# The entry of the MLP in a hybrid decoder layer: normalisation halves on VectorE, two operands built later, a third pair of hidden tiles started early

## The chip, the cores and the metric

The kernel runs on one core of one Trainium2 chip. The metric is device microseconds of one execution; before the change the median of three runs is 1310.89 us (1308.47 to 1311.84). TensorE (PE in the profile) multiplies into PSUM; VectorE (DVE), ScalarE (ACT) and GpSimd (POOL) do the element work; SyncE (SP) only issues DMAs here. Each engine works through its own instructions in order, so an instruction that waits holds up everything behind it on that engine.

## What is computed

One decoder layer on 1024 tokens of width 1024, in float32. Attention and retention run first; the change touches what comes after them:

```python
y = jnp.concatenate([y_ret, y_dsa], axis=-1)
h = h + y @ w_out[l]                                   # output projection
u = rmsnorm(h, norm2_w[l])                             # second norm
h = h + jnp.square(jax.nn.relu(u @ w_ff1[l])) @ w_ff2[l]   # MLP, 1024 -> 4096 -> 1024
```

## The kernel before

**Precision.** A float32 operand is split in a high half (a rounded copy, made by ScalarE) and a low half (operand minus high half, a subtraction). A product is then three matmuls: high by high, high by low, low by high. Names that end in `h` and `l`, or begin with `wh` and `wl`, are such halves.

**The output projection** (`out_mm`, L689) takes 24 matmuls per block of 128 tokens and column half `ch`: eight slices `d` of `y`, three matmuls each (L694 to L696). Its weights for one column half are loaded as four raw tiles of two slices (`wr`, three buffers) and split into `ow[0]`. `out_prep` loads the four tiles `ys` of a block from DRAM. The list `todo` (last piece of column half 0, then the eight blocks of column half 1) is worked through one after the other.

**The second norm** (`norm2`, L875 on) of block `b` runs between the blocks of the output projection, by `norm_step`. When both column halves of block `b` are in `hrow` (L702), ScalarE squares and sums (L879), GpSimd makes the reciprocal root (two tiny operations, L141 and L142), VectorE scales into `un` (L881), TensorE transposes `un` in eight pieces into two PSUM tiles `tps[0]` and `tps[1]` (L889), and ScalarE and VectorE build from these the operands of the MLP.

**The MLP's first product** uses a scheme with seven products in place of eight, on halves of the tokens (blocks 0 to 3 and 4 to 7) and of the width. Its token operands are `U[m]`, m = 1 to 7. With `tps` of a block b < 4 called x1, x2 and of the block b + 4 called y1, y2: U[2] = x1 and U[4] = x2 - x1 need the first four blocks alone; U[3] = y1 - y2, U[5] = y2, U[6] = y1 + x1, U[7] = y2 + x2 and U[1] = y2 + x1 need the last four too. `f1` keeps x1 and x2 (`g1`, `g2`). All but U[1] are split inside `norm2`; the low halves of U[4], U[3] and U[6] on GpSimd, those of U[2], U[5] and U[7] on VectorE. U[1] is split at units 3 to 6.

**Pairs and units.** The 4096 hidden rows are worked in 16 pairs `p` of 128-row tiles. A unit (`unit1`) is one product m of one pair: four slices, three matmuls each, 12 in all, and then its share in the four results `C[p, "1a"]`, `"1b"`, `"2a"`, `"2b"` by the table `EVAC`: `1` and `-1` are copies by ScalarE (with a sign), `"+"` and `"-"` additions by VectorE. After the last share of a result (`FIN`) ScalarE applies relu and square. `prep1(n)` builds the weight halves of unit n from the raw tiles (`w1_load`), `AHEAD1` = 4 units ahead. The units stand in the order of `groups`:

```python
groups = [(1, ORD[:2]), (0, ORD), (1, ORD[2:])] + [(p, ORD) for p in range(2, NP)]   # ORD = (2, 4, 3, 5, 6, 7, 1)
```

so products 2 and 4 of pairs 1 and 0, four units that need the first four blocks alone, come ahead of the first product 3.

**What sets the order.** The code is recorded once and a scheduler then places each engine's instructions; the order on an engine can therefore differ from the order of the code, and is fixed in the built program. Semaphores carry the dependences.

Of the kernel before, what the change touches and what calls it, by code (L numbers as in the profile page):

```python
# [81 lines left out]
def layer(ctx, tc, x, meta, norm1_w, w_in, ret_w, q_w, k_w, rel, w_out, norm2_w, w1, w2,  # L82
# [603 lines left out]
    def out_w(ch, alt=False):  # L686
        ow[0] = load_cols(w_out, [(512 * ch, 512)], alt=alt, gain=rgain)
# [188 lines left out]
    def norm2(b, src, u):  # L876
# [15 lines left out]
        def halves(m, x, eng):  # L892
            h, l = [v[:, :, s] for v in U[m]]
            nc.scalar.activation(h, x, AF.Copy)
            eng.tensor_tensor(l, x, h.bitcast(F32), op=SUB)

        def temp():
            return p2["p"].tile([128, 4, 128], F32, tag="yd", name="ut", bufs=4)

        def total(m, x, y, op, eng):  # L900
            t = temp()
            nc.vector.tensor_tensor(t, x, y, op=op)
            halves(m, t, eng)
# [90 lines left out]
    def unit1(n):  # L994
# [10 lines left out]
        for q, how in EVAC[m]:  # L1005
            if how in (1, -1):
                tag, k = ("yd", 4) if q in ("1a", "2b") else ("aop", 6)
                C[p, q] = p2["p"].tile([128, 512], F32, tag=tag, name="c" + q, bufs=k)
                nc.scalar.activation(C[p, q], ps, AF.Copy, scale=float(how))
            else:  # L1010
                c = C[p, q]
                nc.vector.tensor_tensor(c, c, ps, op=ADD if how == "+" else SUB)
                if (q, m) in FIN:
                    nc.scalar.activation(c, c, AF.Relu)
                    nc.scalar.activation(c, c, AF.Square)
                    if q in HELD:
                        nc.sync.dma_start(hid[HELD[q]][:, p], c)
# [147 lines left out]
    for n in range(len(units)):  # L1165
# [56 lines left out]
```

## Time and profile before

| what | value |
|---|---|
| median of three runs | 1310.89 us |
| the profiled execution | 1311.07 us, its span on the core 1309.2 us |
| TensorE busy | 1248.5 us (95%) |
| VectorE busy | 1037.7 us (79%) |
| ScalarE busy | 761.3 us (58%) |
| GpSimd busy | 236.2 us (18%) |
| mean granted TensorE clock | 0.98 of full speed |

The page's first part gives an engine's busy time over the whole span. A view by stretches does the same for chosen pieces of the span, with the granted TensorE clock (1.00 is 2.4 GHz) and the load on the DMA engines. The view of waits sums the idle time of an engine by what ended it. The timeline lists instructions with their start; a bracket gives the idle time ahead of one and what ended it. Starts of matmuls that follow each other closely are the reliable figure there; their durations overlap.

### The profile page before, as it was taken

Reading aid. Unit: us, or ns where it says so; the run is one execution under the profiler, and the core shown is the slowest. Engines: PE = TensorE matmul, PEld = TensorE weight load, DVE = VectorE, ACT = ScalarE, POOL = GpSimd, SP = SyncE. Lnnn points to the kernel's source line nnn. Section 1 sums busy time; section 2 is a strip of 40 time slices with the busy share of each in tenths; the row PEclk is TensorE's granted clock in tenths of the full one; section 3 lists DMA queues with packets and bytes.
Section 4 is the critical chain, followed back from the end, with each engine's and each line's share of the span. In section 5 each row is a group of like instructions: output and inputs, shape, how many; then the busy total and the mean of one; then the engine's idle time right before and its main releaser. Section 6 shows DMA issues by size and latency. Waiting matters only on the chain.

```text
span 1309.2 us, 18365 instructions
## 1 busy us (share of the span) xinstructions
PE 1248.5 (95%) x6032; PEld 1031.6 (79%) x6032; DVE 1037.7 (79%) x2297; ACT 761.3 (58%) x1612; POOL 236.2 (18%) x286
## 2 busy tenths in 40 slices
PE   5999989999999899999997999999999999999998
PEld 4888867777887677877786888888888888888887
DVE  5579999995459889976579887777788887887875
ACT  6567556787975777764356565555455444444442
POOL 4002373425244332200233000000000100000000
PEclk8999989999999899999998999999999999999999
DMA  8103031202021322212963444434539834344222
GB/s 277 61 18 91 17 97 63 74 9 73 9 73 39 131 98 83 84 60 89 324 225 119 169 145 153 145 145 144 186 129 345 327 112 181 137 153 173 94 95 97
DMA packets 101278, 165.05 MB, mean 126 GB/s; under 512 B 8712, under 2 KB 48944, under 8 KB 97472
## 3 DMA queue, kind: packets, MB, share of 16 engines
q1 hardware_dynamic: 101184, 163.90, 36.3%
q8 instruction: 47, 0.77, 0.2%
q14 instruction: 47, 0.39, 0.1%
HBM read 113.46 MB, written 51.85 MB: 126 GB/s over the span
## 4 chain that ended last, share of the span: by engine, by line
PE 69%; DVE 18%; ACT 5%; issue 3%; DMA 2%; POOL 1%; SPq 0%; ACTq 0%; DVEq 0%; POOLq 0%
PE psB L1121 5%; PE psB L1120 5%; PE psB L1122 5%; PE psB L1002 4%; PE psB L1003 4%; PE psB L1004 4%; PE psA L1003 4%; PE psA L1002 4%; PE psA L1004 4%; PE psA L246 3%; PE psA L247 3%; PE psA L248 3%; PE psA L1121 3%; PE psA L1120 3%; PE psA L1122 3%
## 5 line engine op out<-in xcount | busy, mean ns | idle before, releaser
L973 ACT ACTIVATE wh<-ga 128x512 fp32r<-128x512 f32 x144 | 87.5, 628 | 164.0 <-PE psB L1121 143.1
L246 PE MATMUL psA<-wh,uh 128*128 128x512 f32 x376 | 152.4, 406 | 2.9 <-DVE fg L487 2.2
L247 PE MATMUL psA<-wh,ul 128*128 128x512 f32 x376 | 150.1, 399 | 0.0
L248 PE MATMUL psA<-wl,uh 128*128 128x512 f32 x376 | 149.8, 399 | 0.0
L974 DVE TENSOR_TENSOR wl<-ga,wh 128x512 fp32r<-128x512 f32 x144 | 96.7, 688 | 49.4 <-ACT wh L973 48.8
L973 ACT ACTIVATE wh<-sum 128x512 fp32r<-128x512 f32 x128 | 78.8, 625 | 71.6 <-DVE sum L970 61.0
L751 ACT ACTIVATE jk_top<-sc,tcand 128x784 bf16<-128x784 f32 (+2 forms) x93 | 98.3, 1057 | 24.4 <-DVE tcand L821 20.3
L1121 PE MATMUL psB<-wh,wl 128*128 128x512 f32 x280 | 108.9, 389 | 0.0
L1122 PE MATMUL psB<-wl,wh 128*128 128x512 f32 x280 | 108.9, 389 | 0.0
L1120 PE MATMUL psB<-wh 128*128 128x512 f32 x280 | 106.8, 389 | 0.0
L974 DVE TENSOR_TENSOR wl<-sum,wh 128x512 fp32r<-128x512 f32 x128 | 88.6, 693 | 4.7 <-ACT wh L973 4.7
L246 PEld LDWEIGHTS psA<-wh,uh 128*128 128x128 f32 x376 | 71.9, 191 | 16.9 <-DVE fg L487 1.9
L248 PEld LDWEIGHTS psA<-wl,uh 128*128 128x128 f32 x376 | 71.7, 191 | 14.0
L247 PEld LDWEIGHTS psA<-wh,ul 128*128 128x128 f32 x376 | 71.8, 191 | 12.5
L1040 POOL COPY ga<-wl 128x1 f32<-128x1 f32 x8 | 6.6, 827 | 400.3 <-PE psB L1003 276.3
L746 DVE TENSOR_SCALAR_CACHE_REDUCE jk_cnt<-sc,tcand 128x400 bf16<-128x400 f32 (+2 forms) x93 | 70.3, 756 | 1.0
L359 ACT ACTIVATE rl<-psB,absw 128x320 f32<-128x320 f32 (+5 forms) x104 | 53.1, 556 | 31.0 <-DVE sc L363 16.8
L1121 PE MATMUL psA<-wh,wl 128*128 128x512 f32 x168 | 65.4, 389 | 0.0
L1122 PE MATMUL psA<-wl,wh 128*128 128x512 f32 x168 | 65.4, 389 | 0.0
L1120 PE MATMUL psA<-wh 128*128 128x512 f32 x168 | 64.9, 389 | 0.0
L194 POOL TENSOR_TENSOR wl<-wr,wh 128x512 fp32r<-128x512 f32 x44 | 61.3, 1419 | 19.0 <-ACT wh L189 15.6
L363 DVE SCALAR_TENSOR_TENSOR sc<-rl,sgnw,sc 128x320 f32<-128x320 f32 (+5 forms) x91 | 56.1, 651 | 8.2 <-ACT rl L359 7.2
(391 smaller groups left out, 3582.0 us busy)
## 6 DMA issues: line engine op xcount, KB each, us to landing
ga<-hid SPq DMA_DIRECT2D x28, 1024.0 KB, 5.2
wr<-in_w_ff_dram SPq DMA_DIRECT2D x34, 512.0 KB, 4.9
hid<-hs SPq DMA_DIRECT2D x48, 256.0 KB, 2.0
wr<-in_w_in_dram SPq DMA_DIRECT2D x32, 256.0 KB, 3.1
ysd<-ys SPq DMA_DIRECT2D x32, 256.0 KB, 2.4
ys<-ysd SPq DMA_DIRECT2D x32, 256.0 KB, 5.0
gb<-in_w_ff_dram SPq DMA_DIRECT2D x8, 1024.0 KB, 5.3
ga<-in_w_ff_dram SPq DMA_DIRECT2D x8, 1024.0 KB, 5.0
```

The source lines that it names most:

```text
L246: nc.tensor.matmul(ps[:P, :n], uh, wh, start=d == 0, stop=False)
L247: nc.tensor.matmul(ps[:P, :n], ul, wh, start=False, stop=False)
L248: nc.tensor.matmul(ps[:P, :n], uh, wl, start=False, stop=d == 7)
L751: nc.scalar.activation(jk_top[:, :ncol[i]], sc[i], AF.Sign, scale=-1.0, bias=cand[:, j:j + 1], accum_out=cnt[:, j:j + 1])
L973: nc.scalar.activation(view(hi), s, AF.Copy)
L974: nc.vector.tensor_tensor(view(lo), s, view(hi).bitcast(F32), op=SUB)
L1002: nc.tensor.matmul(ps, hi[:, a], uh[:, d], start=d == 0, stop=False)
L1003: nc.tensor.matmul(ps, lo[:, a], uh[:, d], start=False, stop=False)
L1004: nc.tensor.matmul(ps, hi[:, a], ul[:, d], start=False, stop=d == 3)
L1120: nc.tensor.matmul(ps[tb], ah[:, t], bh, start=j == 0 and m not in CONT, stop=False, skip_group_check=True)
L1121: nc.tensor.matmul(ps[tb], al[:, t], bh, start=False, stop=False, skip_group_check=True)
L1122: nc.tensor.matmul(ps[tb], ah[:, t], bl, start=False, stop=j == NO - 1, skip_group_check=True)
```

## The change

It is made of six edits.

1. `norm2`: the low halves of U[4], U[3] and U[6] are subtracted on VectorE, none on GpSimd (`halves` has no engine argument any more). GpSimd keeps L141 and L142.
2. `norm2`: U[7] and U[1] are no longer split there and at units 3 to 6; their sums stay in `f1` (`g2` takes y2 + x2 in place). A new function `late_halves` splits them at units 5 to 8, two blocks per unit. A small GpSimd copy that reads the last low half of U[3] and writes into U[7] and U[1] stands ahead of it.
3. `groups`: products 2 and 4 of pair 2 come right behind those of pair 1, so six units stand ahead of the first product 3; the raw weights of pair 2 are loaded twice.
4. `EVAC` and `FIN`: products 2 and 4 are copied out alone, by ScalarE, as `"1b"` and `"1a"`; at product 3 VectorE makes `"2b"` (product 3 minus `"1b"`) and adds `"1a"` to `"1b"`, which is then finished. Per pair ScalarE has three copies in place of four, VectorE as many operations as before, one of them between SBUF tiles.
5. The raw weights of the output projection's second half are loaded ahead of the last block of the first half, and split between the load of the next block.
6. The first raw tiles of the MLP and the first two `prep1` are called up to two blocks earlier.

```diff
-            eng.tensor_tensor(l, x, h.bitcast(F32), op=SUB)
+            nc.vector.tensor_tensor(l, x, h.bitcast(F32), op=SUB)
...
-            total(4, tps[1], g1, SUB, nc.gpsimd)
+            nc.vector.tensor_tensor(t, tps[1], g1, op=SUB)
+            halves(4, t)
         else:
+            nc.scalar.activation(t, tps[0], AF.Copy)
+            nc.vector.tensor_tensor(t, t, tps[1], op=SUB)
+            halves(3, t)
+            halves(5, tps[1])
             t = temp()
-            nc.scalar.activation(t, tps[0], AF.Copy)
-            total(3, t, tps[1], SUB, nc.gpsimd)
-            halves(5, tps[1], nc.vector)
-            total(6, tps[0], g1, ADD, nc.gpsimd)
-            total(7, tps[1], g2, ADD, nc.vector)
+            nc.vector.tensor_tensor(t, tps[0], g1, op=ADD)
+            nc.vector.tensor_tensor(g2, tps[1], g2, op=ADD)
             nc.vector.tensor_tensor(g1, tps[1], g1, op=ADD)
+            halves(6, t)
+
+    def late_halves(m, tb):
+
+        s = slice(128 * tb, 128 * tb + 128)
+        h, l = [v[:, :, s] for v in U[m]]
+        x = f1[m == 7][:, tb]
+        nc.scalar.activation(h, x, AF.Copy)
+        nc.vector.tensor_tensor(l, x, h.bitcast(F32), op=SUB)
...
-    EVAC = {2: [("1b", 1), ("2b", -1)], 4: [("1b", "+"), ("1a", 1)], 3: [("2a", 1), ("2b", "+")], 5: [("2a", "+"), ("1a", "-")],
+    EVAC = {2: [("1b", "=")], 4: [("1a", "=")], 3: [("2a", "="), ("2b", "1b"), ("1b", "1a")], 5: [("2a", "+"), ("1a", "-")],
             6: [("2b", "+")], 7: [("1a", "+")], 1: [("1a", "+"), ("2b", "+")]}
-    FIN = {("1b", 4), ("2a", 5), ("1a", 1), ("2b", 1)}
+    FIN = {("1b", 3), ("2a", 5), ("1a", 1), ("2b", 1)}
-    groups = [(1, ORD[:2]), (0, ORD), (1, ORD[2:])] + [(p, ORD) for p in range(2, NP)]
+    groups = [(1, ORD[:2]), (2, ORD[:2]), (0, ORD), (1, ORD[2:]), (2, ORD[2:])] + [(p, ORD) for p in range(3, NP)]
...
+    for g in range(3):
+        w_out_raw(g)
     for k, (ch, b) in enumerate(todo):
         if k == 1:
-            out_w(1, True)
-        nxt = out_prep(*todo[k + 1]) if k < NB else None
+            ow[0] = [], []
+            for g in range(4):
+                if g == 1:
+                    nxt = out_prep(*todo[k + 1])
+                    w_out_raw(3)
+                w_out_split(g)
+        else:
+            nxt = out_prep(*todo[k + 1]) if k < NB else None
...
-        if k == 6:
+        if k == 5:
             w1_load(0, 0)
             w1_load(0, 1)
-
-    for n in range(2):
-        prep1(n)
+        if k in (6, 7):
+            prep1(k - 6)
...
-        if 3 <= n < 7:
-            s = slice(128 * (n - 3), 128 * (n - 3) + 128)
-            nc.scalar.activation(U[1][0][:, :, s], f1[0][:, n - 3], AF.Copy)
-            nc.vector.tensor_tensor(U[1][1][:, :, s], f1[0][:, n - 3], U[1][0][:, :, s].bitcast(F32), op=SUB)
+        for m, n0 in ((7, 5), (1, 7)):
+            if n == n0:
+                nc.gpsimd.tensor_copy(U[m][0][:, 0, 0:512:128], U[3][1][:, 0, 384:388].bitcast(F32))
+            for tb in (2 * (n - n0), 2 * (n - n0) + 1):
+                if 0 <= tb < 4:
+                    late_halves(m, tb)
```

What it makes of the order in the built programs, at three places. The number behind a name tells buffers apart; they differ between the two programs.

**TensorE where the output projection goes over to column half 1.** `psB_7381` collects block 0 and `psB_7413` block 1; `wh_7368` (before) and `wh_7373` (after) come from the fourth raw weight tile. Before:

```order
L694 MATMUL psB_7381<-wh_7362,ys_5240 128x512
L695 MATMUL psB_7381<-wh_7362,ys_5240 128x512
L696 MATMUL psB_7381<-wl_7363,ys_5240 128x512
L694 MATMUL psB_7381<-wh_7368,ys_5240 128x512
L695 MATMUL psB_7381<-wh_7368,ys_5240 128x512
L694 MATMUL psB_7413<-wh_7338,ys_5236 128x512
```

After, the end of block 1's twelve rows and what follows:

```order
L696 MATMUL psB_7413<-wl_7358,ys_5236 128x512
L694 MATMUL psB_7413<-wh_7361,ys_5236 128x512
L695 MATMUL psB_7413<-wh_7361,ys_5238 128x512
L696 MATMUL psB_7413<-wl_7362,ys_5236 128x512
L696 MATMUL psB_7381<-wl_7370,ys_5240 128x512
L694 MATMUL psB_7381<-wh_7373,ys_5240 128x512
L695 MATMUL psB_7381<-wh_7373,ys_5240 128x512
```

The 12 matmuls of block 1's first four slices, which stood behind the first use of the fourth raw tile, now stand ahead of it.

**TensorE ahead of the first product 3** (`u3h`). The two rows with `ident` are the transposes of block 7. Before:

```order
L1004 MATMUL psB_7871<-u2l_7122,wh_7808 128x512
L889 MATMUL psB_7888<-ident_85,un_7423 128x128 x4
L889 MATMUL psB_7893<-ident_85,un_7423 128x128 x4
L1002 MATMUL psB_7946<-u2h_7121,wh_7855 128x512
L1003 MATMUL psB_7946<-u2h_7121,wl_7856 128x512
L1004 MATMUL psB_7946<-u2l_7122,wh_7855 128x512
```

Twelve matmuls of the unit `psB_7946` follow them, then the first `u3h`. After:

```order
L1012 MATMUL psA_7989<-u4l_7124,wh_7903 128x512
L889 MATMUL psB_7880<-ident_85,un_7423 128x128 x4
L889 MATMUL psB_7885<-ident_85,un_7423 128x128 x4
L1010 MATMUL psB_7926<-u2h_7121,wh_7843 128x512
L1011 MATMUL psB_7926<-u2h_7121,wl_7844 128x512
L1012 MATMUL psB_7926<-u2l_7122,wh_7843 128x512
```

Here two whole units, 24 matmuls (`psB_7926`, `psB_7968`), follow the transposes before the first `u3h`. From the end of the output projection to that row there are 48 matmuls and 24 transposes before (blocks 5 to 7), 71 matmuls and 17 transposes after (the transposes of block 5 and the first matmul of a unit have moved ahead of the last half block of the projection).

**VectorE ahead of the sum for U[3] of block 7** (`ut_7900` before, `ut_7890` after). Before:

```order
L1012 TENSOR_TENSOR c1b_7884<-c1b_7884,psA_7921 128x512
L895 TENSOR_TENSOR u7l_7278<-ut_7800,u7h_7277 128x4x128
L1173 TENSOR_TENSOR u1l_7866<-f1_7125,u1h_7865 128x4x128 x2
L970 TENSOR_TENSOR sum_8043<-wr1_7853,wr1_7996 128x512
L895 TENSOR_TENSOR u5l_7272<-psB_7831,u5h_7271 128x4x128
L902 TENSOR_TENSOR ut_7848<-psB_7831,f1_7126 128x512
L970 TENSOR_TENSOR sum_8065<-wr1_7853 128x512
L917 TENSOR_TENSOR f1_7125<-psB_7831,f1_7125 128x512
L902 TENSOR_TENSOR ut_7900<-ut_7898,psB_7893 128x512
```

After:

```order
L881 SCALAR_TENSOR_TENSOR un_7423<-hrow_7268,rs_y_7814,nrow2_2087 128x1024
L895 TENSOR_TENSOR u5l_7272<-psB_7793,u5h_7271 128x4x128
L914 TENSOR_TENSOR f1_7126<-psB_7793,f1_7126 128x512
L915 TENSOR_TENSOR f1_7125<-psB_7793,f1_7125 128x512
L909 TENSOR_TENSOR ut_7828<-ut_7828,psB_7823 128x512
L913 TENSOR_TENSOR ut_7835<-psB_7818,f1_7125 128x512
L978 TENSOR_TENSOR sum_7985<-wr1_7853 128x512
L982 TENSOR_TENSOR wl_7963<-sum_7964,wh_7962 128x512
L895 TENSOR_TENSOR u3l_7274<-ut_7828,u3h_7273 128x4x128
L895 TENSOR_TENSOR u5l_7272<-psB_7823,u5h_7271 128x4x128
L914 TENSOR_TENSOR f1_7126<-psB_7823,f1_7126 128x512
L915 TENSOR_TENSOR f1_7125<-psB_7823,f1_7125 128x512
```

with `ut_7890` right behind. From the addition that completes block 7's rows (L702) to this sum there are 25 rows before, one of them the wide `un` and four the low halves of U[7] and U[1]; after there are 22, two of them wide, and those low halves stand behind the last low half of U[3].

## Rows read from the trace of the kernel before

**Rows 1.** Page, part 1: busy us (share of the span) and instructions of TensorE and VectorE

```profile
PE 1248.5 (95%) x6032; PEld 1031.6 (79%) x6032; DVE 1037.7 (79%) x2297; ACT 761.3 (58%) x1612; POOL 236.2 (18%) x286
```

**Rows 2.** Stretches: length, busy us of each engine (instructions), PEclk, DMA share, GB/s

```profile
630.00:640.00 10.00, 7.80 (x32) 5.34 (x30) 2.47 (x4) 1.45 (x3) 2.22 (x2) 1.00 0.99 346
...
690.00:700.00 10.00, 5.61 (x20) 3.97 (x19) 10.00 (x13) 6.57 (x13) 6.93 (x4) 0.73 0.65 212
700.00:710.00 10.00, 6.89 (x21) 5.16 (x21) 10.00 (x17) 7.89 (x14) 2.28 (x2) 0.76 0.14 52
...
800.00:900.00 100.00, 100.00 (x443) 82.81 (x442) 76.69 (x123) 53.66 (x99) 0.00 (x0) 1.00 0.42 147
```

**Rows 3.** Waits of TensorE from 590 to 1001 us: us in total, times, longest

```profile
PE psB L1002 <- ACT u3h L894: 3.1, 1, 3.1
PE psB L889 <- DVE un L881: 1.9, 1, 1.9
PE psB L694 <- ACT wh L189: 1.3, 1, 1.3
PE psB L1002 <- DVE ut L902: 1.3, 1, 1.3
PE psB L889 <- DVE f L917: 1.2, 1, 1.2
PE psB L694 <- DMA ys<-ysd: 0.8, 1, 0.8
...
PE psB L695 <- DMA ys<-ysd: 0.8, 1, 0.8
```

**Rows 4.** Timeline of TensorE: start, duration, line, operands, count [idle before, ended by]

```profile
680.80 1.03 PE L889 MATMUL psB<-ident,un 128*128 128x128 f32 x8
681.59 0.48 PE L1002 MATMUL psA<-u4h,wh 128*128 128x512 f32 x1
...
698.48 0.63 PE L1002 MATMUL psB<-u2h,wh 128*128 128x512 f32 x1
698.91 0.63 PE L1003 MATMUL psB<-u2h,wl 128*128 128x512 f32 x1
...
705.21 0.79 PE L1002 MATMUL psB<-u3h,wh 128*128 128x512 f32 x1 [3.11 <-ACT u3h L894]
...
709.90 0.39 PE L1002 MATMUL psB<-u6h,wh 128*128 128x512 f32 x1
```

**Rows 5.** Timeline of VectorE

```profile
666.37 1.28 DVE L881 SCALAR_TENSOR_TENSOR un<-hrow,rs_y,nrow 128x1024 f32<-128x1024 f32 x1 [2.26 <-POOL rs_y L142]
667.57 0.68 DVE L895 TENSOR_TENSOR u2l<-psB,u2h 128x512 fp32r<-128x512 f32 x1
...
671.68 2.30 DVE L881 SCALAR_TENSOR_TENSOR un<-hrow,rs_y,nrow 128x1024 f32<-128x1024 f32 x1 [1.25 <-POOL rs_y L142]
...
685.01 0.68 DVE L974 TENSOR_TENSOR wl<-wr,wh 128x512 fp32r<-128x512 f32 x1
685.61 0.68 DVE L702 TENSOR_TENSOR hrow<-psB,hp 128x512 f32<-128x512 f32 x1
...
703.82 0.67 DVE L902 TENSOR_TENSOR ut<-ut,psB 128x512 f32<-128x512 f32 x1
```

**Rows 6.** Timeline of GpSimd

```profile
671.61 1.29 POOL L895 TENSOR_TENSOR u4l<-ut,u4h 128x512 fp32r<-128x512 f32 x1
```

**Rows 7.** Timeline of ScalarE around the high half of U[3] of block 7

```profile
704.52 0.63 ACT L894 ACTIVATE u3h<-ut 128x512 fp32r<-128x512 f32 x1
```

**Rows 8.** Groups by line, 640 to 716 us: count | busy us, mean ns | idle before

```profile
L881 DVE SCALAR_TENSOR_TENSOR un<-hrow,rs_y,nrow 128x1024 f32<-128x1024 f32 x8 | 15.4, 1927 | 8.4 <-POOL rs_y L142 8.4
```

**Rows 9.** Timeline of SyncE's DMA issues: start, duration

```profile
627.72 0.42 SPq L214 DMA_DIRECT2D wr<-in_w_out_dram  x1
628.23 0.52 SPq L699 DMA_DIRECT2D ysd<-ys  x1
```

**Rows 10.** DMA issues of 660 to 760 us: count, KB each, median us to landing

```profile
wr<-in_w_ff_dram SPq DMA_DIRECT2D x9, 512.0 KB, 4.5
```

More of the change, by code (lines that the diff above doesn't have):

```diff
@@ L890, in norm2, with halves @@
             tps.append(tp)
-        def halves(m, x, eng):
+        def halves(m, x):
             h, l = [v[:, :, s] for v in U[m]]
             nc.scalar.activation(h, x, AF.Copy)
-            eng.tensor_tensor(l, x, h.bitcast(F32), op=SUB)
+            nc.vector.tensor_tensor(l, x, h.bitcast(F32), op=SUB)
         def temp():
             return p2["p"].tile([128, 4, 128], F32, tag="yd", name="ut", bufs=4)
[L900 to L903, printed above, removed]
         g1, g2 = f1[0][:, b % 4], f1[1][:, b % 4]
+        t = temp()
         if b < 4:
             nc.scalar.activation(g1, tps[0], AF.Copy)
-            halves(2, tps[0], nc.vector)
+            halves(2, tps[0])
             nc.scalar.activation(g2, tps[1], AF.Copy)
-            total(4, tps[1], g1, SUB, nc.gpsimd)
-        else:
+            nc.vector.tensor_tensor(t, tps[1], g1, op=SUB)
+            halves(4, t)
+        else:
+            nc.scalar.activation(t, tps[0], AF.Copy)
+            nc.vector.tensor_tensor(t, t, tps[1], op=SUB)
+            halves(3, t)
+            halves(5, tps[1])
             t = temp()
-            nc.scalar.activation(t, tps[0], AF.Copy)
-            total(3, t, tps[1], SUB, nc.gpsimd)
-            halves(5, tps[1], nc.vector)
-            total(6, tps[0], g1, ADD, nc.gpsimd)
-            total(7, tps[1], g2, ADD, nc.vector)
-            nc.vector.tensor_tensor(g1, tps[1], g1, op=ADD)
+            nc.vector.tensor_tensor(t, tps[0], g1, op=ADD)
+            nc.vector.tensor_tensor(g2, tps[1], g2, op=ADD)
+            nc.vector.tensor_tensor(g1, tps[1], g1, op=ADD)
+            halves(6, t)
[5 more added lines that the diff above has]
+        nc.vector.tensor_tensor(l, x, h.bitcast(F32), op=SUB)
     spread((NB + 1, attend_v(NB - 1, 1)), (9, out_piece(0, 6)))
@@ L1005, in unit1 @@
         for q, how in EVAC[m]:
-            if how in (1, -1):
-                tag, k = ("yd", 4) if q in ("1a", "2b") else ("aop", 6)
+            if (p, q) not in C:
+                tag, k = ("yd", 4) if q[0] == "2" else ("aop", 6)
                 C[p, q] = p2["p"].tile([128, 512], F32, tag=tag, name="c" + q, bufs=k)
-                nc.scalar.activation(C[p, q], ps, AF.Copy, scale=float(how))
+            c = C[p, q]
+            if how == "=":
+                nc.scalar.activation(c, ps, AF.Copy)
+            elif how == "1b":
+                nc.vector.tensor_tensor(c, ps, C[p, how], op=SUB)
+            elif how == "1a":
+                nc.vector.tensor_tensor(c, c, C[p, how], op=ADD)
             else:
-                c = C[p, q]
                 nc.vector.tensor_tensor(c, c, ps, op=ADD if how == "+" else SUB)
[L1013 to L1017, printed above, removed]
+            if (q, m) in FIN:
+                nc.scalar.activation(c, c, AF.Relu)
+                nc.scalar.activation(c, c, AF.Square)
+                if q in HELD:
+                    nc.sync.dma_start(hid[HELD[q]][:, p], c)
         if m == 1:
@@ L1144, in layer, with w_out_raw, w_out_split @@
     pre = out_prep(*todo[0])
+    wraw = {}
+    def w_out_raw(g):
+        wraw[g] = wp.tile([128, 2, 512], F32, tag="wr", name="wr", bufs=3)
+        nc.sync.dma_start(wraw[g], w_out[256 * g:256 * g + 256, 512:].rearrange("(j p) w -> p j w", p=128))
+    def w_out_split(g):
+        for j in range(2):
+            d = 2 * g + j
+            for v, k in zip(split(wraw[g][:, j], 512, True, rgain[:, d:d + 1] if d < 4 else None), range(2)):
+                ow[0][k].append(v)
+    for g in range(3):
+        w_out_raw(g)
     for k, (ch, b) in enumerate(todo):
         if k == 1:
-            out_w(1, True)
-        nxt = out_prep(*todo[k + 1]) if k < NB else None
+            ow[0] = [], []
[6 more added lines that the diff above has]
+            nxt = out_prep(*todo[k + 1]) if k < NB else None
         spread((8, out_mm(ch, b, *pre)), *([(1.3, norm_step(b - 1))] if k >= 2 else []))
```

## The prediction

> **What bounds the kernel now.** TensorE is busy for 95% of the span, VectorE for 79% [rows 1], so I looked for the stretches in which TensorE is not at work. In the MLP it works without a gap: 443 matmuls in 100 us, 0.226 us from one to the next at a granted clock of 1.00 [rows 2]. The waits from 590 to 1001 us are few and all lie at the MLP's entry [rows 3]. They make two places.
>
> The first is where the output projection goes over to column half 1: 1.3 us for the split of its fourth raw weight tile and two times 0.8 us for `ys` tiles, 3.0 us in all, while the DMA engines are 99% loaded [rows 2, 3].
>
> The second begins where the projection ends, at 680.80. From there to 709.90 are 29.1 us [rows 4], in which TensorE does 62 matmuls (two units of `u4`, two of `u2`, one of `u3` and two matmuls of `u5`) and 24 transposes. At 0.226 us a matmul and 0.1 us a transpose (eight take 680.80 to 681.59) that is 14.0 + 2.4 = 16.4 us of work, so 12.7 us are lost. Four waits hold 7.5 us of them (3.1, 1.9, 1.3, 1.2), the rest is the clock: 0.73 and 0.76 in the two stretches with the waits [rows 2], a mixture of 2.4 and 1.2 GHz, with 0.43 us from one matmul to the next at 698.48 instead of 0.226 [rows 4]. What TensorE waits for ends in a chain on VectorE, which is busy 10.00 of 10 us in both stretches [rows 2]. Block 7's rows were ready when the projection ended, yet VectorE added them only at 685.61, and came to the sum for `u3h` at 703.82, 18.2 us and 25 rows later [rows 5]; ScalarE's `u3h` follows at 704.52 [rows 7], TensorE at 705.21. So the need is 24.4 us (680.80 to 705.21), the cover 48 matmuls and 24 transposes, 10.8 + 2.4 = 13.2 us.
>
> **The change, part by part.**
>
> *Edit 3, the third pair (cover).* Behind the projection's end there are now 71 matmuls and 17 transposes ahead of the first `u3h`: 16.0 + 1.7 = 17.7 us of cover. The products themselves are not added, they come from later.
>
> *Edits 1 and 2 on VectorE (need).* VectorE gains 12 low halves (U[4], U[3], U[6], four blocks each) at 0.60 us from start to start (685.01 to 685.61, [rows 5]), 7.2 us. Against that, the wide `un` takes 1.28 us at 666.37, from which the next row starts 1.20 later, but 2.30 at 671.68 [rows 5], and there a GpSimd subtraction runs from 671.61 to 672.90 [rows 6]. Over the eight blocks its mean is 1.93 us [rows 8], 5.2 us in all above 8 x 1.28. With no such subtraction on GpSimd I take 1.28 for each. So the move costs VectorE about 2 us net over 60 us, and the chain no longer runs through an operation that takes 1.29 us on GpSimd. The eight low halves of U[7] and U[1] (4.8 us) go behind the last low half of U[3]; four of them stood in the 25 rows. After, from L702 of block 7 to the sum there are 22 rows, two wide: 20 x 0.60 + 2 x 1.20 = 14.4 us. Where L702 starts: between block 5's L702 and block 7's stand two wide rows and 15 others, 2.4 + 9.0 = 11.4 us, plus some 1.5 us for waits of `un` on the chain square, root, scale; TensorE takes 49 matmuls and 15 transposes, 12.6 us, between the same blocks. So VectorE reaches it about 1 us after the projection's end, not 4.8. ScalarE then does `u3h`, 0.63 us [rows 7], behind up to two copies of the same kind: 0.6 to 1.8. Need: 1.0 + 14.4 + 1.7 = 17.1 us, against 17.7 of cover. The wait closes, with 0.6 us to spare.
>
> A rule speaks against edit 1. The Trainium skill (Perfetto Trace Analysis, section Optimizing Scalar/DVE Operations) says that with VectorE saturated it may pay to offload work to GpSimd; here VectorE is saturated and work is taken back from there. The same section warns that the two share an SBUF read port, so that offloading between them might not help, and the pair 1.28 and 2.30 bears out that half. By the first half alone the sum would be that of rival 2.
>
> *Where margins are thin.* The transposes of blocks 3 and 4 now stand whole inside the projection, and each waits for `un`. By the same walk down the rows `un` of block 3 is ready when TensorE arrives, that of block 4 half a microsecond earlier. The sum over pair 0's raw tiles needs a load that SyncE issues only when the split of the second unit has been done; nine VectorE rows, 5.4 us, lie between, against a landing of 4.5 us at the median [rows 10]. Behind a late transpose wait all TensorE rows; behind a late load wait VectorE's L702 of block 7 and all that follows. I leave 1.5 us for such misses with the clock they cost. Bounds: 0, and 6 (three misses of 1 us, each with 1 us of slow clock).
>
> *Edits 2 and 4, late.* The late halves run on VectorE and ScalarE while TensorE does units 3, 5 and 6 of pair 0 (36 matmuls, 8.1 us); on VectorE 4.8 us of halves with five other rows, 3.0 us, lie between the last low half of U[3] and the last of U[1]. Cover 8.1, need 7.8, and TensorE wants the last ones only at the second slice. The small GpSimd copy waits for the last low half of U[3]; ScalarE's late halves are queued behind it, and no other ScalarE row that TensorE wants sooner. Edit 4 takes a copy from ScalarE per pair and adds nothing to VectorE; in the MLP both have room (54 and 77 of 100 us, [rows 2]). Two more raw tiles of 512 KB go under a DMA share of 0.42 [rows 2]. I set these at nothing; if the late halves are 1 us late, they cost that and the clock, 2 us.
>
> *Edits 5 and 6, the projection.* Three of the four raw loads stood early before and stand there still. The fourth moves behind one more store, which waited for GpSimd, and one `ys` load: it is issued at 628.8 instead of 627.72 [rows 9], 1.0 us later. But 12 matmuls of block 1 now stand ahead of its first use, 2.7 us, more than 1.3 + 1.0. That wait goes. The two waits for `ys` follow the landing; one raw tile of 512 KB that was issued ahead of them goes behind, 1.5 us at 346 GB/s [rows 2], while TensorE arrives 1.3 us sooner. Of the 3.0 us I take 2.0 as gained; bounds 0 and 3.0. What is late next is `un` of block 3.
>
> **Sum.** The profiled execution took 1311.07 us (span 1309.2, 1.9 around it), 0.2 above the median of 1310.89; I sum against it. Entry: 12.7 lost before, 1.5 after, gain 11.2. Projection: gain 2.0. Rest: 0, with 1 either way. 1311.07 - 11.2 - 2.0 = 1297.9, say 1298. All 12.7 and 3.0 gained would be 1295.4, the floor; 6 us of misses and nothing in the projection 1304.4.
>
> **The rivals.**
>
> 1. *The wait moves upstream.* A late load for pair 0 or late `un` of blocks 3 to 7 makes TensorE wait again. For it: the margins of 0 to 0.6 us. Against it: the waits per place are short. Two `un` late by 1 us, the load late by 2, each with its slow clock, is 6 to 7 us: 1303 to 1305.
>
> 2. *VectorE pays the full price.* If `un` takes 2.30 us for another reason than GpSimd's subtraction, the two wide rows behind L702 and the two ahead of it add 4 us to the need: 21.1 against 17.7, 3.4 us of wait and some 1.5 of clock: 1311.07 - 2.0 - 12.7 + 5 = 1301.4 to 1303. Against it: 1.28 and 2.30 for the same shape, with GpSimd at work only beside the second [rows 5, 6]. This is what the Trainium skill's advice (Perfetto Trace Analysis, Optimizing Scalar/DVE Operations) would make of the time.
>
> 3. *The norm paces the projection (slower).* TensorE passes a block in 24 matmuls and eight transposes, 6.2 us; the chain from one block's transposes to the next block's `un` (copies, square, root, scale) is near that. If it comes 3 us late in each of five blocks, 3 to 7, with 1.5 us of slow clock each, 22.5 us are lost in place of 12.7: 1311.07 - 2.0 - 12.7 + 22.5 = 1318.9. It decides from about 2 us a block (17.5 us). Against it: VectorE waited 8.4 us in all for the root ahead of the eight `un` [rows 8], while the waits of TensorE for `un` sum to 1.9 us, in one [rows 3].
>
> 4. *It doesn't do what it says.* If the six early units only shift the same waits behind U[5] and U[6], the gain is the projection's or nothing: 1308 to 1311. Against it: the order in the built program has the 24 matmuls behind block 7's transposes.
>
> **Chances.** Forecast (1295.4 to 1302) 0.66; rival 1 0.16; rival 2 0.08; rival 4 0.05; rival 3 0.05. The range 1295 to 1305 holds the forecast and rivals 1 and 2 and leaves out 0.1 and a little on the edges. A measurement tells 0.3% (4 us) from no change. Faster by more than that (below 1307): 0.66 + 0.16 + 0.08 = 0.90; within it 0.05; slower 0.05.
>
> **What would show it.** Right: between the projection's end and the tenth unit TensorE's clock stays at 1.00 and its waits sum to under 2 us; no GpSimd subtraction of 128x512 behind 640 us, and `un` at 1.28 in every block; the wait for the fourth raw tile gone. Wrong: a TensorE wait for `un` inside the projection (rivals 1, 3), `un` at 2.3 us with GpSimd idle (rival 2), a wait of several us ahead of `u3h`, `u7h` or `u1h` (rivals 2, 4), or TensorE below 100 in the MLP's steady stretch, which would mean that edit 4 or the extra loads are not covered.

## The result, and the profile after

The changed kernel takes 1296.80 us (median of four runs, 1296.15 to 1298.06) against 1311.37 us for the kernel before (four runs): a ratio of 0.989, with a 95% interval of 0.9873 to 0.9908, or 14.6 us less. The forecast was 1298 with a range of 1295 to 1305. The profiled execution took 1297.09 us, its span is 1295.1 us; against the profiled 1311.07 us of before that is 13.98 us.

The stretches of the changed kernel (length, busy us of each engine with instructions, PEclk, DMA share, GB/s), to be read against [rows 2]:

```profile
630.00:640.00 10.00, 8.60 (x36) 6.28 (x35) 2.08 (x3) 2.31 (x4) 2.38 (x4) 1.00 1.01 343
...
690.00:700.00 10.00, 9.87 (x48) 7.97 (x47) 10.00 (x18) 7.57 (x15) 0.38 (x2) 1.00 0.11 16
700.00:710.00 10.00, 10.00 (x46) 8.26 (x45) 10.00 (x18) 5.98 (x12) 0.00 (x0) 1.00 0.53 194
...
800.00:900.00 100.00, 100.00 (x442) 82.79 (x442) 79.73 (x128) 54.87 (x98) 0.00 (x0) 1.00 0.46 156
```

Between 690 and 710 us TensorE is now busy for 19.87 of 20 us at a granted clock of 1.00, where it had 12.50 us at 0.73 and 0.76. VectorE is still busy the whole time, but TensorE waits for it only once more, by 0.3 us (below). The steady stretch is as it was. In the view of TensorE's waits from 610 to 720 us only one entry of more than 0.2 us is left (us in total, times, longest), where [rows 3] had seven:

```profile
PE psB L694 <- DMA ys<-ysd: 1.3, 2, 1.0
```

Four timelines show the new race. TensorE at the end of the projection, at the first `u3h` and at the first `u3l`:

```profile
679.59 0.39 PE L696 MATMUL psB<-wl,ys 128*128 128x512 f32 x1
679.82 0.27 PE L889 MATMUL psB<-ident,un 128*128 128x128 f32 x1
...
697.63 0.39 PE L1012 MATMUL psB<-u2l,wh 128*128 128x512 f32 x1
697.86 0.39 PE L1010 MATMUL psB<-u3h,wh 128*128 128x512 f32 x1
...
698.99 0.39 PE L1011 MATMUL psB<-u6h,wl 128*128 128x512 f32 x1
699.51 0.50 PE L1012 MATMUL psB<-u3l,wh 128*128 128x512 f32 x1
```

VectorE from the addition of block 7's rows to the sum for U[3], and to its low half:

```profile
680.59 0.68 DVE L702 TENSOR_TENSOR hrow<-psB,hp 128x512 f32<-128x512 f32 x1
...
687.98 1.28 DVE L881 SCALAR_TENSOR_TENSOR un<-hrow,rs_y,nrow 128x1024 f32<-128x1024 f32 x1 [0.71 <-POOL rs_y L142]
...
695.78 0.67 DVE L909 TENSOR_TENSOR ut<-ut,psB 128x512 f32<-128x512 f32 x1
...
698.78 0.68 DVE L895 TENSOR_TENSOR u3l<-ut,u3h 128x512 fp32r<-128x512 f32 x1
```

ScalarE's high half of U[3] of block 7, and two additions for roots on GpSimd, the second with its power for block 7:

```profile
696.49 0.63 ACT L894 ACTIVATE u3h<-ut 128x512 fp32r<-128x512 f32 x1
```

```profile
648.55 0.19 POOL L141 TENSOR_TENSOR rs_y<-ss,eps 128x1 f32<-128x1 f32 x1 [8.06 <-ACT un L879]
...
683.82 3.50 POOL L141 TENSOR_TENSOR rs_y<-ss,eps 128x1 f32<-128x1 f32 x1 [2.48 <-ACT un L879]
687.40 0.55 POOL L142 TENSOR_TENSOR rs_y<-rs_y,nhalf 128x1 f32<-128x1 f32 x1
```

The high half is ready at 697.12 and TensorE comes for it at 697.86: 0.7 us to spare. The low half is not quite in time: from 698.99 to 699.51 are 0.52 us instead of 0.23, so 0.3 us are lost.

### The profile page after: what moved, and what is told of

It reads as the page before. It is cut to its first block, busy times and chain, and to the rows that moved or that the text cites. A ratio compares the mean times of both kernels' runs of the same rounds, so it can differ in the third digit from the quotient of the medians.

```text
span 1295.1 us, 18360 instructions
## 1 busy us (share of the span) xinstructions
PE 1244.2 (96%) x6032; PEld 1029.4 (79%) x6032; DVE 1035.1 (80%) x2309; ACT 753.8 (58%) x1596; POOL 219.8 (17%) x276
## 4 chain that ended last, share of the span: by engine, by line
PE 69%; DVE 19%; ACT 5%; issue 3%; DMA 2%; POOL 1%; SPq 0%; ACTq 0%; DVEq 0%; POOLq 0%
PE psB L1135 5%; PE psB L1134 5%; PE psB L1133 5%; PE psB L1012 4%; PE psA L1012 4%; PE psA L1010 4%; PE psA L1011 4%; PE psB L1010 4%; PE psB L1011 4%; PE psA L246 3%; PE psA L247 3%; PE psA L248 3%; PE psA L1135 3%; PE psA L1134 3%; PE psA L1133 3%
```

## Experiments

Four kernels undo one edit of the changed kernel each, four put one or two edits alone into the kernel before, and two change the changed kernel further. Each was timed beside the kernel before, whose median was 1311.1 to 1311.6 us in these comparisons. "Gain" is the distance to that median; the whole change gains 14.6. Each 95% interval reaches 1 to 2 us to either side, so two gains that lie less than some 3 us apart are not told apart by the times alone. There is one trace of each kernel, and the traces differ ahead of all edits too: the last matmul of the attention starts between 619.8 and 623.1 us. So what an edit does is read from the place where it acts.

### Edit 3 undone: no third pair

```diff
-    groups = [(1, ORD[:2]), (2, ORD[:2]), (0, ORD), (1, ORD[2:]), (2, ORD[2:])] + [(p, ORD) for p in range(3, NP)]
+    groups = [(1, ORD[:2]), (0, ORD), (1, ORD[2:])] + [(p, ORD) for p in range(2, NP)]
...
-        for m, n0 in ((7, 5), (1, 7)):
+        for m, n0 in ((7, 3), (1, 5)):
```

> The changed kernel with edit 3 undone: two pairs stand ahead of the first product 3, the late halves at units 3 to 6. Behind the projection's end TensorE then has 48 matmuls and 21 transposes, 10.8 + 2.3 = 13.1 us. From L702 of block 7 to the sum for u3h VectorE has 18 rows, two of them wide, 9.6 + 2.4 = 12.0 us (the rows of the third pair's operands are gone too). Theory 1 (need against cover, as in the prediction): 1.0 + 12.0 + 1.7 = 14.7 us of need, so a wait of some 1.6 us ahead of u3h and about 1.5 us of slow clock: 1300 us, 3 above the changed kernel. Theory 2 (the third pair is what closes the wait, the VectorE edits add little): the wait and the clock of the kernel before come back nearly whole, 1306 to 1309. Theory 3 (the VectorE edits alone close it): 1297.

1302.52 us (1302.32 to 1303.89), ratio 0.9937 [0.9922, 0.9952]: gain 8.6, so the third pair is worth 6.0 by the medians. TensorE's waits from 620 to 760 us, and the stretch in which they lie:

```profile
PE psB L1010 <- ACT u3h L894: 3.1, 1, 3.1
PE psB L1012 <- DVE u3l L895: 1.8, 1, 1.8
...
690.00:700.00 10.00, 5.07 (x21) 3.28 (x20) 10.00 (x18) 6.16 (x13) 0.38 (x2) 1.00 0.16 60
```

It lies between theories 1 and 2. The wait ahead of `u3h` is where theory 1 put it, but 3.1 us and not 1.6, and a second one of 1.8 us stands ahead of `u3l`, which I had not priced. Most of the 1.5 us that the first is longer are two terms: L702 of block 7 starts 1.9 us behind the projection's end (680.74 against 678.82) and not 1.0, and the last `un` waits 0.44 us for its root. And 4.9 us of waits close together cost no clock here: it stays at 1.00.

### Edit 2 undone: U[7] and U[1] not held back

```diff
-            nc.vector.tensor_tensor(g1, tps[1], g1, op=ADD)
             halves(6, t)
+            halves(7, g2)
+            nc.vector.tensor_tensor(g1, tps[1], g1, op=ADD)
...
-        for m, n0 in ((7, 5), (1, 7)):
...
+        if 5 <= n < 9:
+            late_halves(1, n - 5)
```

> The changed kernel with edit 2 undone: U[7] is split inside the norm again and U[1] at one block per unit from unit 5, low halves on VectorE, no GpSimd copy. TensorE's cover stays 71 matmuls and 17 transposes, 17.8 us; the scheduler puts 21 rows, two wide, between L702 of block 7 and the sum, three of them low halves of U[7] and U[1]. Theory 1 (need against cover): 1.0 + 13.8 + 1.7 = 16.5 us if L702 itself is not later, so no wait ahead of u3h, and 1297; up to 2.4 us more, with its clock, if the low halves of blocks 4 to 6 push L702 of block 7 back: 1297 to 1301. Theory 2 (holding the late halves back is what matters, five rows or more of VectorE at the wrong place): a wait of 3 us ahead of u3h, 1302.

1299.39 us (1298.12 to 1299.90), ratio 0.9909 [0.9892, 0.9925]: gain 11.7. That is 2.9 less than the whole change, too little for the times alone. TensorE's wait, the stretch behind it, and the last low half of U[3] on VectorE:

```profile
PE psB L1013 <- DVE u3l L895: 2.6, 1, 2.6
...
700.00:710.00 10.00, 9.64 (x35) 7.82 (x36) 10.00 (x18) 4.28 (x8) 0.00 (x0) 0.83 0.31 101
...
699.62 0.68 DVE L895 TENSOR_TENSOR u3l<-ut,u3h 128x512 fp32r<-128x512 f32 x1
```

The time is in theory 1's range and below theory 2's, but the place is another: `u3h` is in time, and the last low half of U[3] is late. It starts 20.0 us behind L702 of block 7 (679.61), against 18.2 us in the changed kernel (680.59 to 698.78): three rows of 0.60 us more, as many as there are low halves of U[7] and U[1] between them. Here a wait of 2.6 us was followed by a stretch at 0.83.

### Edit 1 undone: low halves on GpSimd

```diff
-            nc.vector.tensor_tensor(l, x, h.bitcast(F32), op=SUB)
+            eng.tensor_tensor(l, x, h.bitcast(F32), op=SUB)
...
+            halves(4, t, nc.gpsimd)
+            halves(3, t, nc.gpsimd)
+            halves(6, t, nc.gpsimd)
```

> The changed kernel with edit 1 undone: the low halves of U[4], U[3] and U[6] are subtracted on GpSimd again. Theory 1: the wide row un takes 2.3 us wherever such a subtraction runs beside it and 1.28 elsewhere, a mean near 1.9; the subtractions take 1.3 to 2.8 us each, and the root on GpSimd queues behind them; the last low half of U[3] comes 1.5 to 2.5 us after its high half, while TensorE wants it five matmuls (1.1 us) later: waits of 1 to 3 us with 1.5 us of clock, 1299 to 1302. Theory 2 (GpSimd takes 12 rows, 7.2 us, off a busy VectorE, and the third pair covers the rest): 1296 to 1297.

1300.73 us (1299.13 to 1302.89), ratio 0.9922 [0.9906, 0.9937]: gain 10.4, so edit 1 is worth 4.2 by the medians, although it puts 12 rows back on the engine that is busy all the time. The profiled run is the slowest of the six (1302.89), and not all that it lost hangs on edit 1: after a wait of 1.4 us for a `ys` tile where the projection goes over to column half 1, the granted clock from 640 to 650 us was 0.83, well ahead of the entry. At the entry TensorE lost 2.3 us more than in the changed kernel. TensorE's waits, then GpSimd, then VectorE in the same stretch, then the group of the eight `un` (640 to 716 us):

```profile
PE psB L1012 <- POOL u3l L895: 1.7, 1, 1.7
...
PE psB L1010 <- ACT u3h L894: 0.5, 1, 0.5
PE psB L889 <- DVE un L881: 0.4, 1, 0.4
```

```profile
675.86 2.14 POOL L895 TENSOR_TENSOR u3l<-ut,u3h 128x512 fp32r<-128x512 f32 x1 [1.21 <-ACT u3h L894]
677.96 1.73 POOL L895 TENSOR_TENSOR u6l<-ut,u6h 128x512 fp32r<-128x512 f32 x1
...
699.87 1.29 POOL L895 TENSOR_TENSOR u6l<-ut,u6h 128x512 fp32r<-128x512 f32 x1
701.88 2.79 POOL L895 TENSOR_TENSOR u3l<-ut,u3h 128x512 fp32r<-128x512 f32 x1 [0.72 <-ACT u3h L894]
```

```profile
675.56 1.27 DVE L881 SCALAR_TENSOR_TENSOR un<-hrow,rs_y,nrow 128x1024 f32<-128x1024 f32 x1
676.75 1.79 DVE L982 TENSOR_TENSOR wl<-wr,wh 128x512 fp32r<-128x512 f32 x1
678.47 1.77 DVE L982 TENSOR_TENSOR wl<-sum,wh 128x512 fp32r<-128x512 f32 x1
...
699.88 0.67 DVE L915 TENSOR_TENSOR f<-psB,f 128x512 f32<-128x512 f32 x1
```

```profile
L881 DVE SCALAR_TENSOR_TENSOR un<-hrow,rs_y,nrow 128x1024 f32<-128x1024 f32 x8 | 12.9, 1613 | 4.2 <-POOL rs_y L142 4.2
```

Theory 1 holds, though `un` takes 1.6 us in the mean and not 1.9, and the reason is wider than I had it. Not `un` alone pays: two weight subtractions, both inputs of which are SBUF tiles, take 1.8 us where they take 0.68 elsewhere, and GpSimd's subtraction stretches too (2.14 and 1.73, against 1.29 in [rows 6]). The one that starts second pays: `un` at 675.56, ahead of the subtraction at 675.86, keeps its 1.27, while in [rows 5] and [rows 6] the subtraction started first, at 671.61, and `un` took 2.30. The last `u3l` takes 2.79 us on GpSimd here, and TensorE waits 1.7 us for it. The Trainium skill (SBUF — State Buffer, section SBUF: two separate sides) says that VectorE and GpSimd share a pair of ports; when the VectorE instruction has two SBUF inputs and the GpSimd one reads SBUF, the one that starts first has the pair for its whole length. The rows at 675.56, 676.75 and 678.47 agree, and so do the two at 699.87 and 699.88: there VectorE has an input in PSUM, and both keep their lengths, 0.67 and 1.29.

### Edit 5 undone: the old loading of the projection's second half

```diff
-    for g in range(3):
-        w_out_raw(g)
     for k, (ch, b) in enumerate(todo):
         if k == 1:
+            out_w(1, True)
+        nxt = out_prep(*todo[k + 1]) if k < NB else None
```

> The changed kernel with the new loading of the output projection's second half undone (edit 5). Theory 1: the three waits at the turn come back, 3.0 us against 1.3 now, and nothing else moves: 1298.5 to 1299. Theory 2 (the projection's gain is hidden, since VectorE sets the end of the entry and has its work in either case): 1297, with the lost time taken from slack further on.

1299.03 us (1296.40 to 1301.23), ratio 0.9904 [0.9885, 0.9924]: gain 12.1. That is 2.5 less than the whole change, too little for the times alone, as these runs scatter by 5 us. TensorE's waits from 620 to 760 us are the old ones, and the stretch behind them is slow:

```profile
PE psB L695 <- DMA ys<-ysd: 1.4, 1, 1.4
PE psB L694 <- ACT wh L189: 1.2, 1, 1.2
PE psB L694 <- DMA ys<-ysd: 0.5, 1, 0.5
...
640.00:650.00 10.00, 10.00 (x42) 8.16 (x42) 3.51 (x5) 2.66 (x6) 0.65 (x2) 0.83 1.03 382
```

Theory 1: 3.1 us of waits against 1.3, and none at the entry. The granted clock of 0.83 from 640 to 650 us is a loss that theory 1 did not have; in the kernel before it was 1.00 there behind waits of nearly the same size, 3.0 us.

### Edit 5 alone on the kernel before

```diff
+    for g in range(3):
+        w_out_raw(g)
...
         if k == 1:
-            out_w(1, True)
-        nxt = out_prep(*todo[k + 1]) if k < NB else None
+            ow[0] = [], []
+            for g in range(4):
+                if g == 1:
+                    nxt = out_prep(*todo[k + 1])
+                    w_out_raw(3)
+                w_out_split(g)
```

> The kernel before with edit 5 alone (the new loading of the output projection's second half). Theory 1 (the projection and the entry are two separate terms): 2 us less than before, 1309. Theory 2 (VectorE's work sets when the entry ends, so TensorE only reaches the same waits 2 us sooner): 1311, with the waits ahead of u3h grown by 2 us.

1309.62 us (1308.03 to 1314.05), ratio 0.9990 [0.9979, 1.0001]: a gain of 1.6 that the interval does not tell from none. The waits at the entry:

```profile
PE psB L1002 <- ACT u3h L894: 5.8, 1, 5.8
PE psB L889 <- DVE un L881: 2.1, 1, 2.1
PE psB L1002 <- DVE ut L902: 1.2, 1, 1.2
PE psB L889 <- DVE f L917: 1.0, 1, 1.0
```

They sum to 10.1 us against 7.5 in [rows 3]. So 2.6 us of waiting came back at the entry, and the first `u3h` stands at 704.22, only 1.0 us sooner than in [rows 4]. That 1.0 us is no gain of the edit either: this execution was already 1.2 us ahead when the attention ended (621.27 against 622.44). Theory 2 has the mechanism; whether any of the gain stays, the times do not tell.

### Edits 3 and 4 alone on the kernel before

```diff
-    EVAC = {2: [("1b", 1), ("2b", -1)], 4: [("1b", "+"), ("1a", 1)], 3: [("2a", 1), ("2b", "+")], 5: [("2a", "+"), ("1a", "-")],
+    EVAC = {2: [("1b", "=")], 4: [("1a", "=")], 3: [("2a", "="), ("2b", "1b"), ("1b", "1a")], 5: [("2a", "+"), ("1a", "-")],
...
+    groups = [(1, ORD[:2]), (2, ORD[:2]), (0, ORD), (1, ORD[2:]), (2, ORD[2:])] + [(p, ORD) for p in range(3, NP)]
...
-        if 3 <= n < 7:
+        if 5 <= n < 9:
```

> The kernel before with edits 3 and 4 alone (third pair and the results kept apart; U[7] and U[1] split as before, low halves on GpSimd as before). TensorE's cover is 72 matmuls and 18 transposes, 18.2 us. Theory 1 (need against cover): L702 of block 7 comes 4.8 us behind the projection's end as before, then 24 rows, one wide, 15.0 us, then 1.4 us of ScalarE: 21.2 us, 3.0 us of wait ahead of u3h and up to 1.7 for the low half on GpSimd, with 0 to 2 us of slow clock: 4.7 to 6.7 lost in place of 12.7, so 1303 to 1305. Theory 2 (cover bought with early units does nothing while VectorE runs late): 1309 to 1311. Theory 3 (the third pair is all): 1299, as the whole change without the projection's part.

1303.94 us (1302.01 to 1305.31), ratio 0.9937 [0.9923, 0.9952]: gain 7.3, inside theory 1. One wait is left at the entry; 3.0 us ahead of `u3h` and up to 1.7 for its low half were priced, and the wait is the first alone, 1.1 us longer:

```profile
PE psB L1002 <- ACT u3h L894: 4.1, 1, 4.1
```

Two terms are off and largely cancel: L702 of block 7 starts 2.2 us behind the projection's end (684.00 against 681.81) and not 4.8, and from there to the sum for U[3] (703.02) are 19.0 us and not 15.0.

### Edits 1 and 2 alone on the kernel before

```diff
-        def halves(m, x, eng):
+        def halves(m, x):
...
+        for m, n0 in ((7, 3), (1, 5)):
+            if n == n0:
+                nc.gpsimd.tensor_copy(U[m][0][:, 0, 0:512:128], U[3][1][:, 0, 384:388].bitcast(F32))
+            for tb in (2 * (n - n0), 2 * (n - n0) + 1):
+                if 0 <= tb < 4:
+                    late_halves(m, tb)
```

> The kernel before with edits 1 and 2 alone (low halves on VectorE, U[7] and U[1] held back to units 3 to 6); two pairs ahead, results evacuated as before. TensorE's cover is 48 matmuls and 24 transposes, 13.4 us. Theory 1 (need against cover): 1.0 + 13.8 + 1.7 = 16.5 us, so 3.1 us of wait ahead of u3h and about 1.8 ahead of u3l as without the third pair, 4.9 us with 0 to 2 us of slow clock in place of 12.7: 1303 to 1305.5. Theory 2 (GpSimd's work comes back to a saturated VectorE, and only the third pair makes room for it): no gain or a loss, 1310 to 1314.

1305.15 us (1304.46 to 1305.71), ratio 0.9949 [0.9937, 0.9962]: gain 6.1, inside theory 1's range, but partly by luck. The waits come to 5.1 us against 4.9 expected, with a granted clock of 0.88 and 0.78 in the two stretches from 690 us:

```profile
PE psB L1009 <- ACT u3h L894: 4.5, 1, 4.5
...
PE psB L1011 <- DVE u3l L895: 0.6, 1, 0.6
...
681.65 0.68 DVE L702 TENSOR_TENSOR hrow<-psB,hp 128x512 f32<-128x512 f32 x1
```

The sum of the waits hides two misses: 4.5 us ahead of `u3h` where 3.1 were priced, since L702 of block 7 starts 3.7 us behind the projection's end (677.95) and not 1.0, and 0.6 ahead of `u3l` where 1.8 were. Counted as in the prediction, TensorE lost 9.6 us at the entry, not 4.9 to 6.9; of the 6.1 us between the two profiled executions 2.6 were there already when the attention ended (619.83 against 622.44).

### Edit 4 alone on the kernel before

```diff
-    FIN = {("1b", 4), ("2a", 5), ("1a", 1), ("2b", 1)}
+    FIN = {("1b", 3), ("2a", 5), ("1a", 1), ("2b", 1)}
...
+            if how == "=":
+                nc.scalar.activation(c, ps, AF.Copy)
+            elif how == "1b":
+                nc.vector.tensor_tensor(c, ps, C[p, how], op=SUB)
+            elif how == "1a":
+                nc.vector.tensor_tensor(c, c, C[p, how], op=ADD)
```

> The kernel before with edit 4 alone (products 2 and 4 copied out alone, their sums made at product 3). Between L702 of block 7 and the sum for u3h stand 25 rows in place of 26, so 0.6 us less of need; ScalarE has one copy less per pair. Theory 1 (edit 4 is only what lets three pairs lie open at once and moves one row out of the way): 1310.5, within 0.6 of before. Theory 2 (edit 4 itself loosens VectorE or ScalarE in the whole MLP): 1308 or less. Theory 3 (the sum of two SBUF tiles at product 3 delays the later pairs): 1313 or more.

1311.18 us (1310.09 to 1312.42), ratio 0.9997 [0.9988, 1.0006]: no change, theory 1. The first `u3h` stands at 705.26 against 705.21 in [rows 4]. That the edit pays by letting a third pair lie open is argued from the code: no run has edit 3 without edit 4.

### Four VectorE rows more in the changed kernel

```diff
         else:
+            if b >= 6:
+                for _ in range(2):
+                    nc.vector.tensor_tensor(t, g1, g2, op=ADD)
             nc.scalar.activation(t, tps[0], AF.Copy)
```

> The changed kernel with four VectorE rows more (two each in the norms of blocks 6 and 7: f1 + f1 into the temporary tile, overwritten right after). The scheduler makes 28 rows of the 22 between L702 of block 7 and the sum for u3h; TensorE's cover is unchanged at 17.8 us. Theory 1 (need against cover, with a margin of 0.7 us at u3h in the changed kernel): 6 x 0.60 - 0.7 = 2.9 us of wait, and 0 to 2 us of slow clock: 1299.5 to 1302. Theory 2 (the margin is wider than the rows show, since VectorE idles 0.7 us for the root there and other rows can step aside): 1296.8 to 1297.5.

1300.92 us (1300.16 to 1302.47), ratio 0.9918 [0.9904, 0.9932]: 3.9 us of the gain are gone. TensorE's wait, and the stretch behind it:

```profile
PE psB L1013 <- ACT u3h L894: 3.4, 1, 3.4
...
700.00:710.00 10.00, 10.00 (x38) 7.64 (x37) 10.00 (x18) 6.08 (x12) 0.38 (x2) 0.83 0.49 182
```

Six rows more ahead of the sum, less the 0.7 us to spare, were to give 2.9 us of wait; it is 3.4, and a stretch at 0.83 behind it. The rest is L702 of block 7, which starts 1.4 us behind the projection's end (679.12 against 677.75) where it was 0.8. The margin is as thin as the rows say, and theory 2 falls.

### The MLP's first raw tiles issued later

```diff
+        if after is not None:
+            nc.gpsimd.tensor_copy(raw[:, 0, 0:1], after[:, 0:1])
...
-            w1_load(0, 0)
-            w1_load(0, 1)
+            w1_load(0, 0, hrow[1][:, 0])
+            w1_load(0, 1, hrow[1][:, 0])
```

> The changed kernel with its first MLP raw tiles issued later: a GpSimd copy of one column from un of block 2 into each tile stands ahead of the load, so that they no longer lie on the DMA queue among the ys tiles of blocks 0 and 1. Theory 1 (the ys tiles are late because 512 KB tiles for the MLP are issued ahead of them while the DMA engines are full): the 1.3 us of waits for ys go, 1295.5 to 1296. Theory 2 (the DMA engines are full in any case, the same bytes only change places): 1296.8, the wait stays or moves to a later ys tile or to the first weights of the MLP, whose raw tiles now land after 660 us: up to 1300.

1298.53 us (1297.43 to 1300.05), ratio 0.9899 [0.9884, 0.9915]: no gain, where theory 1 had 1.3 us; that the median is 1.7 us above the changed kernel's is within the scatter. The waits for `ys` become one, at 643.58 us instead of 632 and 638:

```profile
PE psB L694 <- DMA ys<-ysd: 2.2, 1, 2.2
```

Theory 2 fits: a wait for `ys` stays and has moved to a later tile. None of the ten kernels is faster than the changed one.

## Why the prediction was right, point by point

**The place and its sum.** The two losses were where the rows put them, and both nearly closed. Of the 13.98 us between the two profiled executions the projection gave 1.9: it ends at 679.82 instead of 680.80, and seven transposes and one matmul more, 0.9 us, lie ahead of that end. Forecast: 2.0. The entry gave nearly all the rest: counted as in the prediction, over the matmuls and transposes up to 729 us, TensorE loses 0.8 us there in place of 12.8 (12.7 in the prediction, which counted up to 709.90). Forecast: 11.2 won, 12.0 measured.

**Need against cover.** Counted from the projection's end, `u3h` was forecast ready at 17.1 us and is ready at 17.3; TensorE was forecast there at 17.7 and comes at 18.0. That the need came out within 0.2 us is partly luck, as its terms missed both ways: L702 of block 7 starts 0.8 us behind the end (forecast 1.0), the 22 rows take 15.2 us (14.4), of which 0.71 is a wait of `un` for its root that I had only allowed for ahead of L702, and the sum and ScalarE's `u3h` behind it take 1.3 us (1.7). A margin of 0.6 us is smaller than the largest of these misses. (The 22 count L702 itself and the 25 of before do not; counted alike they are 22 and 26.) The low half of U[3], which I had not followed, is the one that is 0.3 us late. In the four kernels where the same count expected a wait ahead of `u3h`, one came, each time longer: 3.4 us for 2.9 with four rows more, 4.1 for 3.0 with edits 3 and 4 alone, 4.5 for 3.1 with edits 1 and 2 alone, 3.1 for 1.6 without the third pair. The count has the place and the mechanism, and is 0.5 to 1.5 us too low; the term that is hardest to get is where L702 of block 7 starts.

**Edit 1.** `un` is 1280 ns in the mean over all eight blocks against 1927 in [rows 8], without a subtraction on GpSimd: rival 2 has no row left. With the subtractions put back it is 1613. The reason that I gave, that the price is `un`'s, was too narrow, as the weight subtractions at 1.8 us show. The Trainium skill's first advice (Perfetto Trace Analysis, Optimizing Scalar/DVE Operations), to offload a saturated VectorE, would have cost time here, 4.2 us by the medians and 2.3 at the entry in the traces; its warning behind it is what the runs bear out.

**Margins.** None of the misses came: no wait of TensorE for `un` (rivals 1 and 3), none for pair 0's load. The residual of 1.5 us was set too high by 0.7. Behind it lay a price of 1 us of slow clock for 1 us of wait, which is not a price at all: 4.9 us of waits without the third pair left the granted clock at 1.00, 5.1 us with edits 1 and 2 alone were followed by stretches at 0.88 and 0.78, and one wait of 2.6 us in the second experiment by a stretch at 0.83. That, the root's 0.71 us and the split of the need above are the mis-sized terms.

**The projection as a term of its own.** In the sum I added it to the entry. That holds only since the entry closed: alone on the kernel before, the same edit won 1.7 us at the turn to column half 1 and put 2.6 us more waiting at the entry.

**Edits 2 and 4.** Edit 4 at nothing: 1311.18 alone, right. Edit 2 I had counted as a matter of its own later end; undone it costs a wait of 2.6 us and the clock behind it, through the low half of U[3], which the rows of U[7] and U[1] push back. Edit 6 was not taken out by itself, so its worth is open.

**How the gain divides.** The medians cannot divide it: undone one at a time, third pair, VectorE halves, holding back and new loading cost 6.0, 4.2, 2.9 and 2.5 us, each known to some 3 us, and only the first two are clear of that. The traces show the places. The table has the time that TensorE lost beyond 0.226 us a matmul and 0.1 us a transpose, in one execution of each kernel: at the turn (626 to 660 us) and at the entry (from the projection's end to 729 us). The figures are good to some 0.3 us.

| kernel | gain of the medians | lost at the turn | lost at the entry |
|---|---|---|---|
| before | 0 | 4.5 | 12.8 |
| changed | 14.6 | 2.7 | 0.8 |
| edit 3 undone | 8.6 | 2.6 | 6.5 |
| edit 2 undone | 11.7 | 2.8 | 4.7 |
| edit 1 undone | 10.4 | 4.7 | 3.1 |
| edit 5 undone | 12.1 | 5.8 | 0.5 |
| edit 5 alone | 1.6 | 2.8 | 14.8 |
| edits 3 and 4 alone | 7.3 | 6.0 | 6.4 |
| edits 1 and 2 alone | 6.1 | 4.2 | 9.6 |
| edit 4 alone | 0.4 | 4.8 | 12.7 |
| four rows more | 10.7 | 3.1 | 5.6 |
| raw tiles later | 12.7 | 5.3 | 0.3 |

Edits 1, 2 and 3 act at the entry, and none of them closes it without the others; edit 5 acts at the turn, and alone it is taken back at the entry. The parts do not simply add up: alone, edits 3 and 4 save 6.4 us at the entry and edits 1 and 2 save 3.2, together with the rest of the change 12.0. In four of the traces (edits 1 and 5 undone, edits 3 and 4 alone, raw tiles later) the granted clock from 640 to 650 us, behind the turn, is 0.83 or 0.84, and in the other eight 1.00. In the first and the third of them the loading at the turn is that of the kernel they are held against, so a part of their times is not the edit's.

## What to carry to other kernels

Where an in-order engine is busy all the time, count two things from the moment at which the consumer would arrive: the rows that the producer still has ahead of the operand, and the work that the consumer has ahead of it; the wait is the difference, for the low half as well as for the high one. Early work of the consumer and fewer or later rows of the producer count alike, and neither engine's busy share shows it. What the clock adds is not in the count: here 4.9 us of waits cost none, and 5.1 us in another kernel some 3 us more. A gain ahead of an open wait came back here as waiting.

## What was not expected of the hardware

The GpSimd addition of 128x1 ahead of the root took 0.19 us at 648.55 and 3.50 us at 683.82 in the changed kernel. It ended at 687.32. VectorE ran rows with SBUF operands alone from 683.58 to 687.27, one behind the other:

```profile
683.58 0.68 DVE L982 TENSOR_TENSOR wl<-sum,wh 128x512 fp32r<-128x512 f32 x1
684.18 1.28 DVE L982 TENSOR_TENSOR wl<-wr,wh 128x512 fp32r<-128x512 f32 x2
685.38 0.68 DVE L982 TENSOR_TENSOR wl<-sum,wh 128x512 fp32r<-128x512 f32 x1
685.99 0.68 DVE L895 TENSOR_TENSOR u3l<-ut,u3h 128x512 fp32r<-128x512 f32 x1
686.59 0.68 DVE L978 TENSOR_TENSOR sum<-wr 128x512 f32<-128x512 f32 x1
```

So GpSimd got its turn only when VectorE stopped, not between two of its rows, and VectorE then waited 0.71 us for the very root. The Trainium skill (SBUF — State Buffer, section SBUF: two separate sides) speaks of one instruction that holds the ports; here six in a row did. That the rows on VectorE are the cause is read from these times; no run took them away. With edit 2 undone the addition took 3.31 us at 682.44 in the same way. But with edit 1 undone it took 0.52 us in the midst of such rows (GpSimd, then VectorE):

```profile
688.19 0.52 POOL L141 TENSOR_TENSOR rs_y<-ss,eps 128x1 f32<-128x1 f32 x1 [1.22 <-ACT un L879]
...
687.98 0.68 DVE L982 TENSOR_TENSOR wl<-sum,wh 128x512 fp32r<-128x512 f32 x1
688.58 1.28 DVE L982 TENSOR_TENSOR wl<-wr,wh 128x512 fp32r<-128x512 f32 x2
```

So rows in a row can keep GpSimd out, but do not always; what decides it is open.
